# A decoder block's start with x loaded twice: by token for the sums of squares, by feature for the projections

## Chip, cores and metric

The kernel runs on one NeuronCore of one Trainium2 chip. The metric is the device time of one execution in microseconds (us). Before the change the median of three runs is 838.75 us (838.01 to 840.37).

## The reference

One layer of a decoder trunk on 512 tokens of 1024 features, in float32. What matters here is its beginning and one side product:

```python
h = rmsnorm(x, g_pre_mix)                  # x * rsqrt(mean(x*x over features) + 1e-6) * g
ca, cb, q, k, v, pu, gl = split_cols(h @ w_in)
...
bias = rel_bias[rel_bucket(dist)]          # added to the attention logits
...
x = x + sigmoid(x @ w_ple_gate) * (p @ w_ple_proj)
```

The whole of `h @ w_in` waits for the RMS norm, the norm for the sum over all features of each token's squares. `p @ w_ple_proj` needs no norm and only the embedding `p`.

## The kernel before

All activations lie with features on the partitions and the 512 tokens along the free axis: `x` is eight tiles `x_t[kt]` of 128x512, 256 KB each. Weights come as chunks of 128x1024 (512 KB, `raw`), in the order in which they are used. Each chunk is split by ScalarE into a rounded high part `wh` (line 90, a cast) and by VectorE into the low rest `wl` (line 94). Activations are split in the same way by `mul_split` (lines 149 and 150). A product then takes three matmuls, high by high, high by low and low by high (`mm3`, lines 154 to 156).

The part up to `start.close()` stands in an order written by hand; behind it a scheduler with a simulated time line places the instructions, and it may put them anywhere between the hand-ordered ones that it follows. Each engine executes its own list strictly in its order, so an instruction that waits holds everything behind it on its engine. SyncE (SP) issues nearly all loads, GpSimd (POOL) the stores `proj_d` to DRAM and the copies of the attention bias.

The start goes like this. Eight warm-up matmuls (line 192) run while the first data travel. SP issues half of chunk 0, the two tiles of `p`, the other half, four tiles of `x`, half of chunk 1, four tiles of `x`, the other half, then the small parameters `par_sb` (128x493, line 177), `rb_sb` and `oh_sb` (lines 178 and 179, the bias table and its one-hot selector), then chunks 2 and 3. TensorE computes `p @ w_ple_proj` from chunks 0 and 1 (`project_p`, eight output tiles of six matmuls, 48 in all). Meanwhile ScalarE squares each tile of `x` and VectorE adds the squares (`add_square`). The sum over features is a sum over partitions, so TensorE makes it with a column of ones (line 211, in `rstd_steps`), VectorE scales the result, GpSimd raises it to the power -1/2 (line 203), and four transposes by TensorE (line 216) spread it over the partitions. Then, tile by tile, VectorE multiplies `x_t[kt]` by it (line 336), and `mul_split` makes `xnh` and `xnl`, the two parts of the normed input, with the gains from `par_sb`.

The first real use of the normed input is one q tile and one k tile, computed side by side from chunks 2 and 3: 48 matmuls, six for each `kt`, so that each `kt` can start as soon as its `xnh` and `xnl` are there. Ahead of them in TensorE's list stands one small matmul (line 373) that makes the rows of the attention bias from `oh_sb` and `rb_sb`; ScalarE copies them to `rel_r` and GpSimd sends them to DRAM. The scalars of the attention (`lam_s`, `lam_t`, `sub_g`, lines 355 to 368) are computed by VectorE from `par_sb`.

Two limits are written out: `N_RAW` = 3 buffers for raw chunks (a chunk's load waits until the chunk three before it is split; `rel_r` takes a turn in the same three), and at most eight loads of SP in flight, since each waits for the one eight before it.

Of the kernel before, what the change touches and what calls it, by code (L numbers as in the profile page):

```python
# [11 lines left out]
AF = mybir.ActivationFunctionType  # L12
ALU = mybir.AluOpType
# [8 lines left out]

NORM_LAG, WAIT_SUB, WAIT_LN = 10, 4, 8


X_BEFORE_W1, W_EARLY, XN_BEFORE_W3, XN_BEFORE_W4, N_WARM = 3, 2, 2, 7, 8


PACE_OUT, PACE_IN, W_AHEAD = (6, 11), (9, 14), 3
# [5 lines left out]
P = 128  # L35
S = 512
HALF = 256
D = 1024
KT = 8
# [3 lines left out]
EPS = 1e-6  # L43
# [5 lines left out]
DW_W = 32  # L49
# [5 lines left out]
NPAR = CINV + 64  # L55
# [56 lines left out]
def block_kernel(ctx: ExitStack, tc: tile.TileContext, xT, pT, wts, pool_w, par, rel_bias, onehot, out):  # L112
    nc = tc.nc
# [12 lines left out]
    W = Weights(tc, wts, rawp, hlp)  # L126
# [26 lines left out]
    def mm3(o, sh, sl, mh, ml, first, last):  # L153
        nc.tensor.matmul(out=o, lhsT=sh, rhs=mh, start=first, stop=False)  # L154
        nc.tensor.matmul(out=o, lhsT=sh, rhs=ml, start=False, stop=False)  # L155
        nc.tensor.matmul(out=o, lhsT=sl, rhs=mh, start=False, stop=last)  # L156


    start = ExitStack()
    start.enter_context(tc.manual_schedule())  # L160
    p_sb = [act_tile("p") for _ in range(2)]
    x_t = [act_tile("x") for _ in range(KT)]
    par_sb = cp.tile([P, NPAR], F32, name="par_sb")
    rb_sb = cp.tile([32, NH], F32, name="rb_sb")
# [12 lines left out]
    nc.sync.dma_start(out=par_sb, in_=par)
    nc.sync.dma_start(out=rb_sb, in_=rel_bias)
    nc.sync.dma_start(out=oh_sb, in_=onehot)
    W.load(3)  # L180
    mean_mat = cp.tile([P, P], F32, name="mean_mat")
    nc.vector.memset(mean_mat, 1.0 / S)
    ident = cp.tile([P, P], F32, name="ident")
# [3 lines left out]
    neghalf = cp.tile([P, 4], F32, name="neghalf")  # L187
# [18 lines left out]
    def rstd_steps(sq, lo, n, inv_n, got, tag="at"):  # L206


        b = bank(tag)
        for j in range(n):  # L210
            nc.tensor.matmul(out=b[:, j:j + 1], lhsT=sq[:, lo + j * P:lo + (j + 1) * P], rhs=ones_col,  # L211
                             start=True, stop=True)
        r = rstd_from(b[:, 0:n], inv_n, n, "pe")
        yield
        for j in range(n):
            nc.tensor.transpose(out=b[:, j * P:(j + 1) * P], in_=r[:, j:j + 1].to_broadcast([P, P]), identity=ident)  # L216
        got(b[:, 0:n * P])
# [57 lines left out]
    LEFT, RIGHT = slice(0, 512), slice(512, 1024)  # L275
# [4 lines left out]
    p_hl = []  # L280
# [2 lines left out]
        mul_split(h, l, p_sb[kt])  # L283
        p_hl.append((h, l))
    W.split(0, RIGHT)
    ssum = act_tile("ssum")

    def add_square(kt):
        if kt == 0:
            nc.scalar.activation(out=ssum, in_=x_t[0], func=AF.Square)  # L290
        else:
            q = act_tile("sq")
            nc.scalar.activation(out=q, in_=x_t[kt], func=AF.Square)
            nc.vector.tensor_tensor(out=ssum, in0=ssum, in1=q, op=ALU.add)

    proj_d = dr.tile([KT, P, S], F32, name="proj_d")
    banks = {}
# [1 line left out]
    def project_p(m):  # L299
        wh, wl = W.tiles[m // 4]  # L300
        b = banks[m] = bank("mm" if m < 4 or m > 5 else "at")
        for kt in range(2):
            c0 = ((m % 4) * 2 + kt) * P
            mm3(b, wh[:, c0:c0 + P], wl[:, c0:c0 + P], *p_hl[kt], kt == 0, kt == 1)

    stores = []

    def keep_p(m):
        t = act_tile("proj")
        nc.scalar.activation(out=t, in_=banks.pop(m), func=AF.Copy, scale=0.5)  # L310
        stores.append((m, t))

    for m in range(4):
        project_p(m)
        add_square(m)
    for kt in range(4, KT):
        if kt == X_BEFORE_W1 + 1:
            W.split(1, LEFT)
        add_square(kt)
    project_p(4)  # L320
    project_p(5)
    keep_p(0), keep_p(1)
    W.split(1, RIGHT)
    chunk[0] = 2
    x_rB = []
    steps = rstd_steps(ssum, 0, 4, 1.0 / D, x_rB.append)
    next(steps)
    project_p(6)
    W.upto(W_EARLY)
    keep_p(2), keep_p(3)  # L330
    next(steps, None)
    project_p(7)
    xn = []
    for kt in range(KT + 1):
        if kt < KT:
            nc.vector.tensor_tensor(out=x_t[kt], in0=x_t[kt], in1=x_rB[0], op=ALU.mult)  # L336
        if kt > 0:
            h, l = act_tile("xnh", F32R, "xn", xnp), act_tile("xnl", F32R, "xn", xnp)
            mul_split(h, l, x_t[kt - 1], pcol(G_PRE_MIX + kt - 1))
            xn.append((h, l))  # L340
        if kt == XN_BEFORE_W3:
            W.upto(3)
        if kt == XN_BEFORE_W4:
            W.upto(4)
    for m in range(4, KT):
        keep_p(m)
    for m, t in stores:
        nc.gpsimd.dma_start(out=proj_d[m], in_=t)


    lam_t = cp.tile([P, 8], F32, name="lam_t")
# [20 lines left out]
    b = bank("at")  # L372
# [10 lines left out]
                                                      ap=[[0, P], [1, 640]]))  # L383

    repeat_rows(0)

    start.close()


    def project(n, evac, side_by_side=False):  # L390
# [329 lines left out]
    for what in ORDER:  # L720
# [17 lines left out]
        else:  # L738
            m = at_m[what]
# [26 lines left out]
    x_t = []  # L766
# [142 lines left out]
    for quarter in range(4):  # L909
# [58 lines left out]
def _layout(inp):  # L968
    import numpy as np
    g = {k: np.asarray(v) for k, v in inp.items()}  # L970
    f = np.float32

    def feat(a, n):
        return np.ascontiguousarray(a.T.reshape(n, P, S).transpose(1, 0, 2))

    def tiles(w):

        k, m = w.shape
        return w.reshape(k // P, P, m // P, P).transpose(2, 1, 0, 3)

    w_in = g["w_in"][0]
    cols = lambda a, n: w_in[:, a:a + n]
    m_tiles = lambda w: [t.reshape(P, -1) for t in tiles(w)]
    conv_a, conv_b = m_tiles(cols(0, 512)), m_tiles(cols(512, 512))
    q, k = m_tiles(cols(1024, 512)), m_tiles(cols(1536, 512))
    pool = m_tiles(cols(2560, 512))
    gates = m_tiles(cols(3072, 3072))
    v = cols(2048, 512).reshape(KT, P, 512).transpose(1, 0, 2)

    def pairs(w, n):  # L990
        t = tiles(w)
        return [t[i:i + n].transpose(1, 0, 2, 3).reshape(P, -1) for i in range(0, len(t), n)]

    ch = pairs(g["w_ple_proj"][0], 4)
    n_conv = n_qk = 0
    done = [0, 0, 0]
    ys = [pairs(g[n][0], 2) for n in ("w_conv_out", "w_attn_out", "w_pool_out")]
    for what in ORDER:
        if what == "v":
            ch += [v[:, 2 * j:2 * j + 2].reshape(P, -1) for j in range(4)]  # L1000
        elif what == "pool":
            ch += pool
        elif what == "conv":
# [12 lines left out]
    ch += m_tiles(g["w_out"][0])
    w1 = m_tiles(g["w_mlp_in"][0])
    for i in range(4):
        ch += w1[8 * i:8 * i + 8] + m_tiles(g["w_mlp_out"][0][1024 * i:1024 * i + 1024])
    ch += m_tiles(g["w_ple_gate"][0])  # L1020
    wts = np.ascontiguousarray(np.stack(ch))

    par = np.zeros((P, NPAR), f)
    vec = lambda a: a.reshape(-1, P).T
    for c, n in ((G_PRE_MIX, "g_pre_mix"), (G_POST_MIX, "g_post_mix"), (G_PRE_MLP, "g_pre_mlp"),
                 (G_POST_MLP, "g_post_mlp")):
        par[:, c:c + 8] = vec(g[n][0])
    dw = g["conv_dw_w"][0][:, 0, :]
    par[:, DW_W:DW_W + 4 * CW] = dw.reshape(CW, 4, P).transpose(2, 1, 0).reshape(P, -1)
    for c, n in ((DW_B, "conv_dw_b"), (LN_G, "conv_ln_g"), (LN_B, "conv_ln_b"), (POOL_S, "pool_scale")):  # L1030
        par[:, c:c + 4] = vec(g[n][0])
    par[:, SUBLN] = g["subln_g"][0]
    par[:, LAM:LAM + 256] = g["lam_p"][0].reshape(1, 256)
    for i, w in enumerate(WINDOWS):
        par[:, CINV + 16 * i:CINV + 16 * i + 16] = (f(1.0) / np.minimum(np.arange(16) + 1, w).astype(f))[None]

    onehot = np.zeros((32, S), f)
    onehot[_rel_bucket(S - 1 - np.arange(S)), np.arange(S)] = 1.0
    return [feat(g["x"][0], KT), feat(g["p"][0, 0], 2), wts,
            np.ascontiguousarray(g["pool_w"][0].transpose(1, 0, 2).reshape(P, S)), par, np.ascontiguousarray(g["rel_bias"]), onehot]  # L1040


# [25 lines left out]
```

## Time and profile before

| What | us |
|---|---|
| median of 3 runs | 838.75 (838.01 to 840.37) |
| the profiled execution, its own time | 839.83 |
| its span from first to last instruction | 838.1 |
| TensorE busy | 830.9 (99%) |
| VectorE busy | 505.4 (60%) |
| ScalarE busy | 348.6 (42%) |
| GpSimd busy | 30.0 (4%) |

The span is divided among engines that work at the same time, so the shares add up to more than one. TensorE is busy nearly throughout, and the chain that ended last goes through it for 97% of the span. The first 45 us are where the change acts; the rows for them stand further down. Matmul ends are modelled, so neighbouring matmuls overlap in the rows: the distance from start to start tells the pace.

### The profile page before, as it was taken

To read this page: it belongs to the slowest core of one execution; us is meant where nothing else is said; L and a number is where in the kernel's file an instruction comes from. 1 tells how busy PE (TensorE), PEld (TensorE's weight loads), DVE (VectorE), ACT (ScalarE), POOL (GpSimd) and SP (SyncE) were. 2 spreads that over 40 slices of the span, in tenths; PEclk is the share of its full clock that TensorE was granted. 3 is DMA by queue.
4 is the path that set the end of the run, shared out by engine and by line. 5 is a ranking of instruction groups with operands and counts; after the bars stand their busy time and mean duration, and the time that the engine had idled before them with its cause. 6 is when DMAs were issued, how large, how long until landed. Compare 5 with 4: busy or idle time off the path is not lost.

```text
span 838.1 us, 10679 instructions
## 1 busy us (share of the span) xinstructions
PE 830.9 (99%) x4180; PEld 703.6 (84%) x4180; DVE 505.4 (60%) x835; ACT 348.6 (42%) x564; POOL 30.0 (4%) x66
## 2 busy tenths in 40 slices
PE   8999999999999999999999999999999999999998
PEld 7788888888888888888999888888888888889997
DVE  5869669965679985675387631443334434435772
ACT  6734635555452323752446542342233223425341
POOL 2210000010000000000000000000000000000000
PEclk9999999999999999999999999999999999999999
DMA  7463322222222232265203423322223222222311
GB/s 270 152 235 112 113 101 76 79 87 75 76 76 78 99 100 82 95 220 181 76 27 119 158 83 118 101 97 82 98 101 101 100 81 97 100 76 76 127 59 68
DMA packets 27523, 89.11 MB, mean 106 GB/s; under 512 B 3244, under 2 KB 3628, under 8 KB 27472
## 3 DMA queue, kind: packets, MB, share of 16 engines
q1 hardware_dynamic: 26160, 83.95, 29.7%
q0 software_dynamic: 1312, 4.47, 1.6%
q8 instruction: 33, 0.54, 0.3%
q14 instruction: 18, 0.15, 0.1%
HBM read 84.20 MB, written 5.52 MB: 107 GB/s over the span
## 4 chain that ended last, share of the span: by engine, by line
PE 97%; DVE 1%; ACT 0%; DMA 0%; POOL 0%; issue 0%; SPq 0%; ACTq 0%
PE mm L154 21%; PE mm L156 21%; PE mm L155 21%; PE at L154 10%; PE at L155 10%; PE at L156 10%; PE at L211 1%; PE at L457 1%; PE at L455 1%; PE at L488 1%; PE at L216 0%; DMA p<-in_pT_dram 0%; DVE wl L94 0%; POOL per L203 0%; DVE x L336 0%; DVE xnl L150 0%
## 5 line engine op out<-in xcount | busy, mean ns | idle before, releaser
L90 ACT CAST wh<-raw 128x1024 fp32r<-128x1024 f32 (+1 forms) x144 | 148.8, 1038 | 331.2 <-PE mm L155 151.7
L94 DVE TENSOR_TENSOR wl<-raw,wh 128x1024 fp32r<-128x1024 f32 (+1 forms) x144 | 173.3, 1208 | 100.7 <-ACT wh L90 100.3
L156 PE MATMUL mm<-xnh,wl 128*128 128x512 f32 x352 | 137.9, 392 | 0.5 <-DVE wl L94 0.4
L155 PE MATMUL mm<-xnl,wh 128*128 128x512 f32 x352 | 137.6, 391 | 0.0
L154 PE MATMUL mm<-xnh,wh 128*128 128x512 f32 x352 | 137.2, 393 | 0.0
L577 DVE SCALAR_TENSOR_TENSOR acc<-u,par_sb,acc 128x512 f32<-128x512 f32 x116 | 81.3, 742 | 1.2 <-ACT acc L571 1.1
L156 PEld LDWEIGHTS mm<-xnh,wl 128*128 128x128 f32 x352 | 66.1, 188 | 14.6 <-DVE wl L94 1.4
L154 PEld LDWEIGHTS mm<-xnh,wh 128*128 128x128 f32 x352 | 66.1, 188 | 14.2 <-ACT xnh L149 0.9
L155 PEld LDWEIGHTS mm<-xnl,wh 128*128 128x128 f32 x352 | 66.1, 188 | 14.1 <-DVE xnl L150 0.4
L154 PE MATMUL mm<-sh,wh 128*128 128x512 f32 (+1 forms) x152 | 54.4, 358 | 0.0
L155 PE MATMUL mm<-sl,wh 128*128 128x512 f32 (+1 forms) x152 | 54.4, 358 | 0.0
L156 PE MATMUL mm<-sh,wl 128*128 128x512 f32 (+1 forms) x152 | 54.3, 357 | 0.0
L154 PE MATMUL at<-sh,wh 128*128 128x512 f32 (+1 forms) x144 | 53.1, 369 | 0.0
L155 PE MATMUL at<-sl,wh 128*128 128x512 f32 (+1 forms) x144 | 53.0, 368 | 0.0
L156 PE MATMUL at<-sh,wl 128*128 128x512 f32 (+1 forms) x144 | 52.9, 368 | 0.0
L154 PE MATMUL at<-xgh,wh 128*128 128x512 f32 (+1 forms) x144 | 52.8, 367 | 0.0
L155 PE MATMUL at<-xgl,wh 128*128 128x512 f32 (+1 forms) x144 | 52.7, 366 | 0.0
L154 PE MATMUL mm<-xgh,wh 128*128 128x512 f32 (+1 forms) x144 | 52.7, 366 | 0.0
L156 PE MATMUL mm<-xgh,wl 128*128 128x512 f32 (+1 forms) x144 | 52.7, 366 | 0.0
L156 PE MATMUL at<-xgh,wl 128*128 128x512 f32 (+1 forms) x144 | 52.7, 366 | 0.0
L155 PE MATMUL mm<-xgl,wh 128*128 128x512 f32 (+1 forms) x144 | 52.6, 366 | 0.0
L203 POOL TENSOR_TENSOR per<-pec,neghalf 128x4 f32<-128x4 f32 (+1 forms) x11 | 12.3, 1120 | 581.1 <-DVE pec L201 581.1
(251 smaller groups left out, 1537.9 us busy)
## 6 DMA issues: line engine op xcount, KB each, us to landing
raw<-in_wts_dram SPq DMA_DIRECT2D x140, 512.0 KB, 3.2
x<-in_xT_dram SPq DMA_DIRECT2D x16, 256.0 KB, 5.7
proj_d<-proj POOLq DMA_DIRECT2D x8, 256.0 KB, 4.0
proj<-proj_d SPq DMA_DIRECT2D x8, 256.0 KB, 3.9
out_dram<-pg SPq DMA_DIRECT2D x7, 256.0 KB, 2.0
rep_d<-rel_d POOLq DMA_DIRECT2D x4, 320.0 KB, 8.2
raw<-in_wts_dram SPq DMA_DIRECT2D x4, 256.0 KB, 5.2
bias<-rep_d POOLq DMA_DIRECT2D x4, 256.0 KB, 4.1
```

The source lines that it names most:

```text
L90: i = self.nc.scalar.copy(out=wh[:, sl], in_=src)
L94: i = self.nc.vector.tensor_tensor(out=wl[:, sl], in0=src, in1=wh[:, sl].bitcast(F32), op=ALU.subtract)
L154: nc.tensor.matmul(out=o, lhsT=sh, rhs=mh, start=first, stop=False)
L155: nc.tensor.matmul(out=o, lhsT=sh, rhs=ml, start=False, stop=False)
L156: nc.tensor.matmul(out=o, lhsT=sl, rhs=mh, start=False, stop=last)
L203: nc.gpsimd.tensor_tensor(out=r, in0=c, in1=neghalf[:, 0:n], op=ALU.pow)
L211: nc.tensor.matmul(out=b[:, j:j + 1], lhsT=sq[:, lo + j * P:lo + (j + 1) * P], rhs=ones_col, start=True, stop=True)
L455: nc.tensor.matmul(out=lg[m][:, 0:nn], lhsT=q[m][:, cols], rhs=k[m][:, 0:nn], start=True, stop=False)
L457: nc.tensor.matmul(out=lg[m][:, 0:nn], lhsT=ql[m][:, cols], rhs=k[m][:, 0:nn], start=False, stop=True)
L488: nc.tensor.transpose(out=tp[:, j * P:(j + 1) * P], in_=e[:, j * P:(j + 1) * P], identity=ident)
L577: nc.vector.scalar_tensor_tensor(out=t, in0=u[:, k:k + S], scalar=pcol(w0 + k), in1=t, op0=ALU.mult, op1=ALU.add)
```

## The change

`x` becomes a DRAM tensor of sixteen tiles: the eight by feature as before, and behind them the same numbers with tokens on the partitions. The second eight (`x_k`, 2 MB) are loaded first. For each group of 128 tokens ScalarE squares one half of the features with an accumulated sum, VectorE the other half in one instruction, and the mean of squares is there without TensorE's column of ones. The load of `par_sb` is cut in two: its first 32 columns (the gains) stay early, the other 461 come last, behind all of `x`, `rb_sb` and `oh_sb`. Chunk 2 is loaded ahead of the tiles by feature, chunk 3 in their middle. There is one more warm-up matmul, the three matmuls of `project_p` change places among themselves, six of its eight tiles now precede the transposes, and `start.close()` moves up, so that the attention's scalars and the bias matmul are placed by the scheduler.

```diff
-X_BEFORE_W1, W_EARLY, XN_BEFORE_W3, XN_BEFORE_W4, N_WARM = 3, 2, 2, 7, 8
+K_BEFORE_W1, XN_BEFORE_W3, XN_BEFORE_W4, N_WARM = 1, 3, 7, 9
...
+    x_k = [act_tile("xk") for _ in range(2 * 4)]
...
-    for kt in range(KT):
-        nc.sync.dma_start(out=x_t[kt], in_=xT[:, kt, :])
-        if kt == X_BEFORE_W1:
-            W.load(1, halves=True)
+    W.load(1, halves=True)
+    for j in range(2 * 4):
+        nc.sync.dma_start(out=x_k[j], in_=xT[:, KT + j, :])
+        if j == K_BEFORE_W1:
             W.load_half(1, 0)
     W.load_half(1, 1)
-    nc.sync.dma_start(out=par_sb, in_=par)
-    nc.sync.dma_start(out=rb_sb, in_=rel_bias)
-    nc.sync.dma_start(out=oh_sb, in_=onehot)
-    W.load(3)
+    def load_x(kt):
+        nc.sync.dma_start(out=x_t[kt], in_=xT[:, kt, :])
+    nc.sync.dma_start(out=par_sb[:, 0:DW_W], in_=par[:, 0:DW_W])
+    W.load(2)
+    for kt in range(4):
+        load_x(kt)
...
+    for kt in range(4, KT):
+        load_x(kt)
+        if kt == 4:
+            W.load(3)
+    nc.sync.dma_start(out=rb_sb, in_=rel_bias)
+    nc.sync.dma_start(out=oh_sb, in_=onehot)
+    nc.sync.dma_start(out=par_sb[:, DW_W:NPAR], in_=par[:, DW_W:NPAR])
+    half_ms = small(8, "halfms")
+    for j in range(4):
+        if j == 3:
+            W.split(1, LEFT)
+        xa, xb = x_k[2 * j], x_k[2 * j + 1]
+        nc.scalar.activation(out=xa, in_=xa, func=AF.Square, scale=1.0 / math.sqrt(D), accum_out=half_ms[:, j:j + 1])
+        nc.vector.tensor_tensor_reduce(out=xb, in0=xb, in1=xb, op0=ALU.mult, op1=ALU.add, scale=1.0 / D, scalar=0.0,
+                                       accum_out=half_ms[:, 4 + j:5 + j])
+    x_c, x_r = small(4, "xc"), small(4, "xr")
+    nc.vector.scalar_tensor_tensor(out=x_c, in0=half_ms[:, 0:4], scalar=EPS, in1=half_ms[:, 4:8],
+                                   op0=ALU.add, op1=ALU.add)
+    nc.gpsimd.tensor_tensor(out=x_r, in0=x_c, in1=neghalf, op=ALU.pow)
...
-    steps = rstd_steps(ssum, 0, 4, 1.0 / D, x_rB.append)
+    x_rB = bank("at")
+    for j in range(4):
+        nc.tensor.transpose(out=x_rB[:, j * P:(j + 1) * P], in_=x_r[:, j:j + 1].to_broadcast([P, P]), identity=ident)
...
     for m, t in stores:
         nc.gpsimd.dma_start(out=proj_d[m], in_=t)
+    start.close()
...
     repeat_rows(0)
-
-    start.close()
```

Three places show how the lists of the engines change. The first is SP's, the loads behind the second half of chunk 1 (`raw_108` before, `raw_112` now). Before (`raw_118` and `raw_120` are chunks 2 and 3):

```order
L177 DMA par_sb<-in_par_dram 128x493
L178 DMA rb_sb<-in_rel_bias_dram 32x4
L179 DMA oh_sb_98<-in_onehot_dram 32x512
L76 DMA raw_118<-in_wts_dram 128x1024
L76 DMA raw_120<-in_wts_dram 128x1024
```

And now, further down, where the last of the tiles of `x` are (`raw_168` is chunk 3; ahead of these rows stand the first cut of `par_sb`, chunk 2 and four more tiles of `x`):

```order
L179 DMA x_92<-in_xT_dram 128x512
L75 DMA raw_168<-in_wts_dram 128x1024
L179 DMA x_93<-in_xT_dram 128x512
L179 DMA x_94<-in_xT_dram 128x512
L179 DMA x_95<-in_xT_dram 128x512
L295 DMA rb_sb<-in_rel_bias_dram 32x4
L296 DMA oh_sb_98<-in_onehot_dram 32x512
L297 DMA par_sb<-in_par_dram 128x461
```

`rb_sb`, `oh_sb` and most of `par_sb` moved behind two chunks and the eight tiles of `x`.

The second is VectorE's list around the first two tiles of the normed input. Before:

```order
L336 TENSOR_TENSOR x_88<-x_88,at_232 128x512
L336 TENSOR_TENSOR x_89<-x_89,at_232 128x512
L150 SCALAR_TENSOR_TENSOR xnl_270<-x_88,par_sb,xnh_269 128x512
L336 TENSOR_TENSOR x_90<-x_90,at_232 128x512
L150 SCALAR_TENSOR_TENSOR xnl_275<-x_89,par_sb,xnh_274 128x512
```

And now:

```order
L346 TENSOR_TENSOR x_89<-x_89,at_240 128x512
L370 TENSOR_TENSOR lam_s<-par_sb 128x64 x2
L377 TENSOR_SCALAR sub_g<-par_sb 128x1
L381 TENSOR_SCALAR par_sb<-par_sb 128x124
L383 TENSOR_SCALAR ln_half<-par_sb 128x8
L149 SCALAR_TENSOR_TENSOR xnl_266<-x_88,par_sb,xnh_265 128x512
L346 TENSOR_TENSOR x_90<-x_90,at_240 128x512
L386 MEMSET rel_r 4x640
L371 TENSOR_REDUCE lam_t<-lam_s 128x1 x2
L149 SCALAR_TENSOR_TENSOR xnl_275<-x_89,par_sb,xnh_274 128x512
```

The attention's scalars, which read the late part of `par_sb`, moved from behind the last `xnl` to ahead of the first, and the clearing of `rel_r` with two reductions ahead of the second.

The third is TensorE's list between the last matmuls of `project_p` and the first with the normed input. Before:

```order
L155 MATMUL mm_260<-pl_153,wh_144 128x512
L156 MATMUL mm_260<-ph_152,wl_145 128x512
L373 MATMUL at_349<-oh_sb_98,rb_sb 4x512
L154 MATMUL mm_363<-xnh_269,wh_248 128x512
L155 MATMUL mm_363<-xnl_270,wh_248 128x512
```

And now:

```order
L323 MATMUL mm_252<-ph_161,wl_154 128x512
L323 MATMUL mm_252<-pl_162,wh_153 128x512
L388 MATMUL at_350<-oh_sb_98,rb_sb 4x512
L153 MATMUL mm_363<-xnh_265,wh_260 128x512
L154 MATMUL mm_363<-xnl_266,wh_260 128x512
```

The bias matmul kept its place, ahead of all matmuls with the normed input.

## Rows read from the trace of the kernel before

**Rows 1.** The page's part on busy time, by engine.

```profile
PE 830.9 (99%) x4180; PEld 703.6 (84%) x4180; DVE 505.4 (60%) x835; ACT 348.6 (42%) x564; POOL 30.0 (4%) x66
```

**Rows 2.** Stretches: start:end, length; busy us (instructions) by engine; clock, DMA share, GB/s.

```profile
5.53:10.37 4.84, 4.84 (x11) 3.52 (x12) 2.93 (x5) 3.47 (x6) 0.00 (x0) 1.00 0.95 338
...
22.43:34.01 11.58, 11.46 (x49) 8.88 (x49) 11.21 (x20) 8.06 (x13) 1.70 (x4) 1.00 0.31 96
```

**Rows 3.** Time line of TensorE: start, us, instruction, [idle before <-releaser].

```profile
16.28 0.95 PE L211 MATMUL at<-ones_col,ssum 128*128 128x1 f32 x8
...
19.52 0.65 PE L216 MATMUL at<-ident,per 128*128 128x128 f32 x4 [0.80 <-POOL per L203]
...
21.48 1.02 PE L373 MATMUL at<-oh_sb,rb_sb 32*4 32x512 f32 x2
22.43 0.50 PE L154 MATMUL mm<-xnh,wh 128*128 128x512 f32 x1
...
40.49 0.50 PE L156 MATMUL mm<-xnh,wl 128*128 128x512 f32 x1 [0.42 <-DVE wl L94]
```

**Rows 4.** Time line of SP: when each load is issued, and how many.

```profile
8.66 0.33 SPq L81 DMA_DIRECT2D raw<-in_wts_dram  x1
9.29 0.33 SPq L177 DMA_DIRECT2D par_sb<-in_par_dram  x1
...
10.60 0.32 SPq L179 DMA_DIRECT2D oh_sb<-in_onehot_dram  x1
11.23 1.08 SPq L76 DMA_DIRECT2D raw<-in_wts_dram  x2
```

**Rows 5.** Loads issued in short windows, in their order: KB each, us from issue to landing.

```profile
raw<-in_wts_dram SPq DMA_DIRECT2D x1, 256.0 KB, 5.1
...
par_sb<-in_par_dram SPq DMA_DIRECT2D x1, 246.5 KB, 5.5
...
oh_sb<-in_onehot_dram SPq DMA_DIRECT2D x1, 64.0 KB, 4.5
...
raw<-in_wts_dram SPq DMA_DIRECT2D x1, 512.0 KB, 5.0
```

**Rows 6.** A stretch with loads alone, columns as in rows 2.

```profile
7.40:13.80 6.40, 6.40 (x24) 5.08 (x23) 4.74 (x8) 6.25 (x11) 0.00 (x0) 1.00 1.05 398
```

**Rows 7.** Time line of GpSimd: the power and the first four stores.

```profile
17.52 1.95 POOL L203 TENSOR_TENSOR per<-pec,neghalf 128x4 f32<-128x4 f32 x1 [14.50 <-DVE pec L201]
19.41 2.34 POOL L348 DMA_DIRECT2D proj_d<-proj  x4
```

**Rows 8.** DMA queues from 42 to 52 us (q0 GpSimd's, q1 SP's): MB, share of 16 engines.

```profile
DMA packets 922, 3.51 MB, mean 351 GB/s; under 512 B 128, under 2 KB 128, under 8 KB 922
...
q0 software_dynamic: 400, 1.61, 50.2%
q1 hardware_dynamic: 522, 1.90, 48.9%
```

**Rows 9.** Time line of VectorE, from 10 to 60 us.

```profile
21.69 0.75 DVE L150 SCALAR_TENSOR_TENSOR xnl<-x,par_sb,xnh 128x512 fp32r<-128x512 f32 x1 [0.20 <-ACT xnh L149]
...
32.86 0.21 DVE L355 TENSOR_TENSOR lam_s<-par_sb 128x64 f32<-128x64 f32 x1
33.10 0.22 DVE L356 TENSOR_REDUCE lam_t<-lam_s 128x1 f32<-128x64 f32 x1
...
36.96 0.59 DVE L371 MEMSET rel_r<- 4x640 f32 x1
```

**Rows 10.** Time line of ScalarE: four squares; the copy of the bias rows.

```profile
11.23 2.60 ACT L293 ACTIVATE sq<-x 128x512 f32<-128x512 f32 x4
...
37.64 0.58 ACT L374 COPY rel_r<-at 4x512 f32<-4x512 f32 x1
```

**Rows 11.** End of the span: the last matmul; TensorE's stretch after it, columns as in rows 2.

```profile
833.70 0.28 PE L156 MATMUL at<-x2h,wl 128*128 128x256 f32 x1
...
836.50:838.00 1.50, 0.00 (x0) 0.00 (x0) 0.00 (x0) 0.00 (x0) 0.00 (x0) 0.50 0.05 15
```

More of the change, by code (lines that the diff above doesn't have):

```diff
@@ L285, in block_kernel @@
     W.split(0, RIGHT)
[L286 to L294, printed above, removed]
+    for kt in range(4, KT):
[17 more added lines that the diff above has]
+    nc.gpsimd.tensor_tensor(out=x_r, in0=x_c, in1=neghalf, op=ALU.pow)
     proj_d = dr.tile([KT, P, S], F32, name="proj_d")
@@ L303, in project_p @@
             c0 = ((m % 4) * 2 + kt) * P
-            mm3(b, wh[:, c0:c0 + P], wl[:, c0:c0 + P], *p_hl[kt], kt == 0, kt == 1)
+            for z, (w, src) in enumerate(((wh, 0), (wl, 0), (wh, 1))):
+                nc.tensor.matmul(out=b, lhsT=w[:, c0:c0 + P], rhs=p_hl[kt][src], start=kt + z == 0, stop=kt + z == 3)
     stores = []
@@ L311, in keep_p @@
         stores.append((m, t))
-    for m in range(4):
+    for m in range(6):
         project_p(m)
[L315 to L322, printed above, removed]
-    W.split(1, RIGHT)
-    chunk[0] = 2
-    x_rB = []
-    steps = rstd_steps(ssum, 0, 4, 1.0 / D, x_rB.append)
[L327 to L332, printed above, removed]
+    W.split(1, RIGHT)
+    for m in range(2):
+        keep_p(m)
+    x_rB = bank("at")
+    for j in range(4):
+        nc.tensor.transpose(out=x_rB[:, j * P:(j + 1) * P], in_=x_r[:, j:j + 1].to_broadcast([P, P]), identity=ident)
+    chunk[0] = 2
+    for m in range(6, KT):
+        project_p(m)
     xn = []
@@ L335, in block_kernel @@
         if kt < KT:
-            nc.vector.tensor_tensor(out=x_t[kt], in0=x_t[kt], in1=x_rB[0], op=ALU.mult)
+            nc.vector.tensor_tensor(out=x_t[kt], in0=x_t[kt], in1=x_rB, op=ALU.mult)
+        if kt == 0:
+            W.upto(2)
         if kt > 0:
@@ L340, in block_kernel @@
             xn.append((h, l))
+        if kt == 1:
+            keep_p(2), keep_p(3)
         if kt == XN_BEFORE_W3:
@@ L1038, in _layout @@
     onehot[_rel_bucket(S - 1 - np.arange(S)), np.arange(S)] = 1.0
-    return [feat(g["x"][0], KT), feat(g["p"][0, 0], 2), wts,
+    x_rows = g["x"][0].reshape(4, P, D).transpose(1, 0, 2).reshape(P, 8, S)
+    x_both = np.ascontiguousarray(np.concatenate([feat(g["x"][0], KT), x_rows], axis=1))
+    return [x_both, feat(g["p"][0, 0], 2), wts,
             np.ascontiguousarray(g["pool_w"][0].transpose(1, 0, 2).reshape(P, S)), par, np.ascontiguousarray(g["rel_bias"]), onehot]
```

## The prediction, written before the changed kernel was run

> **What bounds the kernel now.** I read the busy times first: TensorE works 830.9 of 838.1 us [rows 1], so all that can be won or lost lies in its few gaps and slow stretches. The stretches of the start come next [rows 2]: between 5.53 and 10.37 us eleven matmuls take 4.84 us, 0.44 each, and from 22.43 to 34.01 us 49 take 11.46, 0.234 each. The first is the pace at 1.2 GHz, the second at 2.4. Then TensorE's time line [rows 3]: the column of ones at 16.28, an idle 0.80 us until GpSimd's power is done, the transposes at 19.52, the bias matmul at 21.48, and at 22.43 the first matmul with the normed input. Behind that it runs nearly without a gap until 40.49, where it had waited 0.42 us for a split of VectorE.
>
> So before the change the start can give back little: the ones (0.95 at most), the idle 0.80 and that 0.42. What can be lost has no such bound: the bias matmul and VectorE's list now stand behind late loads. When the loads land decides the case, and the rows on loads [rows 4 to 8] are the ones to read.
>
> **The squares and the power** leave the path, but buy nothing by themselves. A square by ScalarE took 0.65 [rows 10], and there are four on each engine in place of eight on ScalarE and seven sums on VectorE. I take each at 0.65 to 0.85 for the accumulated sum, an estimate from that row. They follow the loads: the last tile by token stands just ahead of chunk 1's second half, which landed at 8.66 + 5.1 = 13.8 [rows 4, 5]. So it lands near 13.2, its square is done near 14.1, the power, at 1.95 [rows 7], near 16.2. TensorE needs it after 36 matmuls of the embedding, which ended at 16.28 before [rows 3] and end there again: the same loads in the same order feed them. Four transposes (0.65 at most [rows 3]) and twelve matmuls at 0.234 [rows 2] follow without a wait: done near 19.6. Were everything else in place, the bias matmul (0.95, from 21.48 to 22.43 [rows 3]) would let the first normed matmul start at 20.6, 1.9 earlier than before. The ninth warm-up matmul and the other order of the three matmuls lie ahead of this and move nothing.
>
> **The loads.** Up to chunk 1's second half the list carries the same bytes as before: 13.8. Behind it now come 3.2 MB up to `oh_sb`, where there were 0.3 MB. In a stretch with loads alone the chip moved 398 GB/s [rows 6], 0.66 us for a tile of 256 KB. Chunk 2 landed at 11.23 + 5.0 = 16.2, `oh_sb` just before it at 10.60 + 4.5 = 15.1 [rows 4, 5], so a chunk takes 1.13; `par_sb` landed at 9.29 + 5.5 = 14.8, 1.0 after what precedes it, and `rb_sb` and `oh_sb` took 0.3 together. The new sum: 13.8 + 0.15 for the first cut of `par_sb` (0.04 by its 16 KB, 0.3 by the row of `oh_sb`) + two chunks at 1.13 + eight tiles at 0.66 + 0.3 = 21.8 for `oh_sb`, and 22.8 for the late `par_sb`.
>
> That is without the stores. The first four of `proj_d` (256 KB each) were issued from 19.41 on, when no load was in flight [rows 7]; now the first two follow the power at 16.2, the next two near 19, in the midst of the loads. From 42 to 52 us both queues were at work: they divided the engines 50.2 to 48.9, at 351 GB/s together [rows 8]. So the price lies between nothing (all loads first) and 3.4 us (all four stores pass ahead: 2.1 MB at 351 instead of 1.05 MB at 398). I take 2.0, nearer to the upper end, since rows 8 show even sharing but the last two stores start late: **`oh_sb` at 23.8, `par_sb` at 24.8.** The Trainium skill says the same in "DMA: Bandwidth & Descriptors", "Issuing engines are not separate DMA queues": DMAs of all engines run on the same 16 DMA engines and interleave. By that rule the stores cost their full bytes, so 2.6 rather than 2.0, and rows 8 agree with it.
>
> **What waits for them.** TensorE executes its list in order, so the bias matmul waits for `oh_sb` from 19.6 to 23.8, 4.2 us, and all normed matmuls behind it. VectorE waits at `lam_s` for the late `par_sb`; behind it stand the first low part `xnl` and all the rest. Four small instructions (0.21 for a `lam_s` [rows 9], overlapping, 0.6 together) put the first `xnl` at 25.4, against 21.69 [rows 9]: **3.7 late**. The clearing of `rel_r` (0.59) and two reductions (0.22, 0.3 for both [rows 9]) now precede the second `xnl`: **0.9 more**. Then VectorE goes on as before, a product and an `xnl` for each of eight tiles and the split of chunk 3; it was busy 11.21 of those 11.58 us [rows 2], so it cannot catch up, and TensorE ends the first q and k pair 4.6 late. It does not get this back: later it is busy throughout. One stall goes: the wait at 40.49, since the copy of the bias rows (37.64 [rows 10]), which held ScalarE's next cast, and the small work of VectorE are over by then: **minus 0.4**. That makes 4.2. Ends: 1.6 + 0.9 - 0.4, about 2.2, without any store ahead, 5.6 with all four at 351 GB/s.
>
> **The clock.** The last matmul of the span ended at 833.98, and in the stretch from 836.5 on the clock is 0.50, 1.2 GHz [rows 11]: it fell within 2.5 us of the last matmul. TensorE will stand still for 4.2 us from 19.6 and then get a few matmuls at a time until about 28. I take it that it falls to 1.2 GHz there and comes back after a steady stretch like that of the start, eleven matmuls at 0.44 instead of 0.234 [rows 2]: 2.3 us, of which 0.5 pass while VectorE is waited for anyway: **plus 1.8**. Ends: 0 if it stays up, 4 if half pace lasts twice as long. The Trainium skill's "TensorE: Matmul & The Clock Gate" ("HAM oscillation") tells of kernels in which each wait for a DMA between bursts of matmuls brings half rate back; the row at the end of this span agrees.
>
> **Sum.** 3.7 + 0.9 - 0.4 + 1.8 = 6.0. The profiled execution took 839.83, 1.7 around its span, and would take 845.8; it lies 1.1 above the median of the runs. Against that median: 838.75 + 6.0, so **844.7**.
>
> **Rivals.**
> - The waits come, but the clock stays at 2.4 GHz, because the bias matmul and the small bursts are enough. For it: the idle 0.80 at 18.7 changed nothing in the pace [rows 2, 3]. 4.2 us, 843.0.
> - The stores wait behind the loads and the clock stays: `par_sb` at 22.8, 2.2 us, 841.0. Against it: rows 8.
> - Not slower: the loads land before they are missed. It is decided at the bias matmul: `oh_sb` has to be there by 19.6 and the late `par_sb` by 21.1, 0.6 ahead of the first `xnl` of before. Then the normed matmuls start 1.9 earlier and the stall of 0.4 is gone; with a little of the moved 0.9 left over, some 2 us are won: 836.8. Against it: 3.2 MB in the 5.8 us from 13.8 would be 550 GB/s, and rows 6 show 398.
> - The part that the words of the change promise does not happen: the token sums come no sooner, for the squares wait for the same 2 MB as before. That is worth nothing either way, since TensorE waits for `oh_sb` until long after the power.
>
> **How the numbers follow.** The forecast, waits and a fallen clock, gets 0.55, the waits alone 0.27, the light case at 841.0 0.12, the faster case 0.06. A measurement of this kernel tells about 0.3% from no change, 2.5 us: slower begins at 841.3, faster at 836.2. So the first two are slower (0.82, less a little for sizes that come out small), the light case and most of the faster one are within it. The range of 8 in 10 reaches from just under the light case, 840.8, to 847.0, where all four stores pass ahead or the clock comes back late.
>
> **What would show it.** In the changed profile: the bias matmul at about 24 instead of 21.48, after an idle stretch of some 4 us that ends with a DMA; VectorE idle until `lam_s` at about 25, also for a DMA; GpSimd's power before 16.5; the wait of 0.42 near 40 gone or smaller; matmuls at 0.44 apart again somewhere between 23 and 33; the first matmul of the tile after the q and k pair at about 40, against 34.01; and every stretch after 50 us as before, only later. I am wrong if `oh_sb` lands before 20, if VectorE doesn't wait at `lam_s`, or if the late start is won back further on.

## The result and the profile after

The changed kernel takes **844.68 us** (median of 6 runs, 843.77 to 846.38) against 839.12 (838.01 to 840.37, 6 runs) for the kernel before: ratio 1.0069, 95% interval 1.0056 to 1.0081. It is slower by 5.6 us. The profiled execution took 844.38, with a span of 842.6. Over a whole span the mean granted clock is 0.996 in two of the six executions (844.38, the profiled one, and 843.77) and 0.993 in the other four (843.92 to 846.38).

The page's line of busy times, which answers to [rows 1], shows TensorE with as much work as before and 4.5 us more span around it:

```profile
PE 830.0 (99%) x4174; PEld 703.2 (83%) x4174; DVE 503.1 (60%) x836; ACT 346.4 (41%) x564; POOL 29.1 (3%) x66
```

The stretches, with the columns of [rows 2], say where that is:

```profile
22.43:34.01 11.58, 8.13 (x23) 4.85 (x24) 7.80 (x20) 3.69 (x7) 1.96 (x4) 0.71 0.42 155
24.05:30.87 6.82, 4.99 (x9) 2.36 (x10) 4.66 (x14) 2.82 (x5) 0.40 (x1) 0.50 0.28 115
34.01:45.43 11.42, 11.42 (x52) 9.46 (x51) 8.96 (x12) 10.04 (x16) 5.00 (x11) 1.00 0.90 284
```

From 22.43 to 34.01, where 49 matmuls ran before, there are 23, at a mean clock of 0.71; the clock is 0.50, 1.2 GHz, from 24.05 to 30.87. From 34.01 on TensorE is full again. Its time line, for [rows 3]:

```profile
16.46 0.60 PE L339 MATMUL at<-ident,xr 128*128 128x128 f32 x4
...
19.45 0.40 PE L323 MATMUL mm<-pl,wh 128*128 128x512 f32 x1
25.88 1.86 PE L388 MATMUL at<-oh_sb,rb_sb 32*4 32x512 f32 x2 [6.04 <-DMA oh_sb<-in_onehot_dram]
27.67 0.79 PE L153 MATMUL mm<-xnh,wh 128*128 128x512 f32 x1
...
31.89 0.40 PE L153 MATMUL mm<-xnh,wh 128*128 128x512 f32 x1
32.13 0.39 PE L155 MATMUL mm<-xnh,wl 128*128 128x512 f32 x1
...
40.34 0.39 PE L153 MATMUL mm<-xnh,wh 128*128 128x512 f32 x1
...
51.22 0.39 PE L153 MATMUL mm<-wh,xnh 128*128 128x512 f32 x1
```

The transposes no longer wait for the power, and the last matmul of the embedding starts at 19.45. Then TensorE stands for 6.04 us until `oh_sb` is there. 32.13 is the first matmul with the low part of chunk 3, and 40.34 the first one behind the q and k pair, which stood at 34.01 before: 6.33 later. No wait of 0.42 follows. 51.22 is the first matmul of the work behind the next q and k pair. Before, it stood here:

```profile
45.65 0.39 PE L154 MATMUL mm<-wh,xnh 128*128 128x512 f32 x1
```

So the next pair took 10.88 (40.34 to 51.22) instead of 11.64 (34.01 to 45.65): the stall, 0.42 by its row, is worth 0.76 from start to start, and 5.57 of the 6.33 are left. The last matmul starts only 4.62 later (838.32 against 833.70 [rows 11]). The way there from 51.22 took 787.10 us, from 45.65 it took 788.05, and in the traces of the runs below 787.1 to 787.9 with the close in either place; so this looks like spread between executions, and the medians keep 5.6.

VectorE, for [rows 9]:

```profile
26.13 0.36 DVE L370 TENSOR_TENSOR lam_s<-par_sb 128x64 f32<-128x64 f32 x2 [6.61 <-DMA par_sb<-in_par_dram]
...
26.68 0.74 DVE L149 SCALAR_TENSOR_TENSOR xnl<-x,par_sb,xnh 128x512 fp32r<-128x512 f32 x1
...
28.09 0.59 DVE L386 MEMSET rel_r<- 4x640 f32 x1
28.61 0.27 DVE L371 TENSOR_REDUCE lam_t<-lam_s 128x1 f32<-128x64 f32 x2
28.81 0.73 DVE L149 SCALAR_TENSOR_TENSOR xnl<-x,par_sb,xnh 128x512 fp32r<-128x512 f32 x1
...
30.73 1.21 DVE L93 TENSOR_TENSOR wl<-raw,wh 128x1024 fp32r<-128x1024 f32 x1
```

It waits 6.61 us at `lam_s` for the late cut of `par_sb`; the first `xnl` comes at 26.68 instead of 21.69 [rows 9]. The last row is the split of chunk 3. Two rows of VectorE in the kernel before belong beside these, the second `xnl` and its split of chunk 3:

```profile
22.95 0.75 DVE L150 SCALAR_TENSOR_TENSOR xnl<-x,par_sb,xnh 128x512 fp32r<-128x512 f32 x1
23.62 1.22 DVE L94 TENSOR_TENSOR wl<-raw,wh 128x1024 fp32r<-128x1024 f32 x1
```

GpSimd, for [rows 7], and SP's last small loads, for [rows 4]:

```profile
14.79 1.03 POOL L311 TENSOR_TENSOR xr<-xc,neghalf 128x4 f32<-128x4 f32 x1 [11.77 <-DVE xc L309]
15.80 1.29 POOL L362 DMA_DIRECT2D proj_d<-proj  x2
19.32 1.07 POOL L362 DMA_DIRECT2D proj_d<-proj  x2 [2.23 <-ACT proj L329]
```

```profile
17.67 0.34 SPq L296 DMA_DIRECT2D oh_sb<-in_onehot_dram  x1
18.32 0.35 SPq L297 DMA_DIRECT2D par_sb<-in_par_dram  x1
```

`oh_sb` is issued at 17.67 and used at 25.88; four stores and the last tiles of `x` share the DMA engines with it.

### The profile page after: what moved, and what is told of

The parts are those of the page before. It is cut to its first block, busy times and chain, and to the rows that moved or that the text cites. A ratio compares the mean times of both kernels' runs of the same rounds, so it can differ in the third digit from the quotient of the medians.

```text
span 842.6 us, 10669 instructions
## 1 busy us (share of the span) xinstructions
PE 830.0 (99%) x4174; PEld 703.2 (83%) x4174; DVE 503.1 (60%) x836; ACT 346.4 (41%) x564; POOL 29.1 (3%) x66
## 4 chain that ended last, share of the span: by engine, by line
PE 96%; DMA 3%; DVE 0%; SPq 0%; issue 0%; ACT 0%
PE mm L153 21%; PE mm L154 21%; PE mm L155 21%; PE at L153 10%; PE at L154 10%; PE at L155 10%; DMA oh_sb<-in_onehot_dram 1%; DMA xk<-in_xT_dram 1%; PE at L216 1%; DMA x<-in_xT_dram 1%; PE at L470 1%; PE at L468 1%; PE at L501 1%; DMA p<-in_pT_dram 1%; PE at L221 0%; PE at L388 0%
## 5 line engine op out<-in xcount | busy, mean ns | idle before, releaser
L153 PEld LDWEIGHTS mm<-sh,wh 128*128 128x128 f32 x152 | 28.5, 188 | 4.5
```

## The experiments

The theory was that of the prediction: TensorE waits for `oh_sb` and VectorE, at the moved `lam_s`, for the late `par_sb`; the stores make both loads later, and the clock adds to it. The rivals: the double load of `x` itself costs, or one of the waits is harmless. Each kernel was run in five rounds beside the kernel before, whose medians then were 838.5 to 838.9. The edits are against the changed kernel, if nothing else is said; a mark for all of them is the start of the first matmul behind the pair (34.01 before, 40.34 in the change). The table's numbers are those of the paragraphs below; runs 3, 4 and 9 to 11 have other edits and stand only there.

| Kernel | small loads | close of the first pool | median us | ratio to before (95%) |
|---|---|---|---|---|
| the change | `oh_sb`, `par_sb` last | moved up | 844.68 | 1.0056 to 1.0081 |
| 2 | `oh_sb`, `par_sb` last | old place | 843.25 | 1.0040 to 1.0064 |
| 5 | `oh_sb` early, `par_sb` last | moved up | 846.28 | 1.0078 to 1.0109 |
| 6 | `oh_sb` early, `par_sb` last | old place | 837.93 | 0.9984 to 1.0001 |
| 1 | all early | moved up | 844.90 | 1.0058 to 1.0082 |
| 7 | all early | old place | 839.06 | 0.9993 to 1.0010 |
| 8 | those of before, `x` once | moved up | 843.72 | 1.0053 to 1.0085 |

**1. All small parameters early.**

```diff
     nc.sync.dma_start(out=par_sb[:, 0:DW_W], in_=par[:, 0:DW_W])
+    nc.sync.dma_start(out=rb_sb, in_=rel_bias)
+    nc.sync.dma_start(out=oh_sb, in_=onehot)
+    nc.sync.dma_start(out=par_sb[:, DW_W:NPAR], in_=par[:, DW_W:NPAR])
     W.load(2)
```

> The changed kernel with rb_sb, oh_sb and the late cut of par_sb loaded right behind the first cut, ahead of chunk 2 and of x by feature; x is still loaded twice. If the wait for these small loads is the cause, the bias matmul starts near 19.7 us instead of 25.9, VectorE does not stop for lam_s, and the time falls from 844.7 to between 838 and 840.5. If the second load of x itself is the cause (x by feature lands too late), the normed matmuls only wait elsewhere and the time stays at 842.5 or more.

Measured 844.90: a miss. The scheduler, which now saw `par_sb` early, put `lam_s` still further ahead, in front of chunk 0's second split. VectorE waits there, and TensorE for the split, first VectorE's row and then TensorE's:

```profile
14.83 0.36 DVE L370 TENSOR_TENSOR lam_s<-par_sb 128x64 f32<-128x64 f32 x2 [7.46 <-DMA par_sb<-in_par_dram]
```

```profile
15.85 0.80 PE L323 MATMUL mm<-ph,wl 128*128 128x512 f32 x1 [6.32 <-DVE wl L93]
```

So a wait had only changed its place, and this run can't tell what the loads cost.

**2. The old close.**

```diff
-    start.close()
...
     repeat_rows(0)
+
+    start.close()
```

> The changed kernel with start.close() back at its old place: the attention's scalars and the clearing of rel_r stand behind the last xnl on VectorE, the loads are as in the change. If VectorE's wait at lam_s is the bound, the normed matmuls come early and the time falls to 840 or less. If TensorE's wait for oh_sb is enough by itself, the bias matmul still starts near 25.9, the first normed matmul near 27.7, the q and k pair ends near 40, and the time is 844 to 845.5.

Measured 843.25, between the two forecasts. `lam_s` stands behind the last `xnl` again and waits for nothing, but TensorE still stands before the bias matmul:

```profile
23.88 1.86 PE L387 MATMUL at<-oh_sb,rb_sb 32*4 32x512 f32 x2 [4.43 <-DMA oh_sb<-in_onehot_dram]
25.67 0.79 PE L153 MATMUL mm<-xnh,wh 128*128 128x512 f32 x1
...
38.58 0.39 PE L153 MATMUL mm<-xnh,wh 128*128 128x512 f32 x1
...
45.06 0.50 PE L155 MATMUL mm<-xnh,wl 128*128 128x512 f32 x1 [0.42 <-DVE wl L93]
```

So most of the loss is there without any wait at `lam_s`: the wait for `oh_sb` makes it, together with the clock that falls in it. The clock's part: the bias matmul takes 1.79 us to the next start, 0.95 before [rows 3], and the 48 matmuls of the pair 12.91 (25.67 to 38.58) instead of 10.95 at 0.228 (the pace of the change from 32.13 to the mark), together 2.8. The wait itself ends only 2.40 later than the bias matmul of before. And the stall of 0.42 is back, as it should be if the moved work of VectorE and ScalarE had removed it.

**3. The stores last.**

```diff
-    for m, t in stores:
+    for m, t in reversed(stores):
```

> The changed kernel with the eight stores of proj_d issued in reverse, so that GpSimd sends none before the bias rows: no store shares the DMA engines with the loads. If the stores delay the loads, oh_sb lands near 22 instead of 25.7 and par_sb near 23, and the time falls by some 3 us, to 841 to 842.5. If they wait their turn behind the loads, nothing moves: 844 to 845.

The tile that is ready last now heads the stores, and the others stand behind it in GpSimd's list, so all of them follow the loads. Measured 843.14 (ratio 1.0037 to 1.0061): below the change, but short of the 841 to 842.5 expected. TensorE and VectorE:

```profile
22.86 1.01 PE L388 MATMUL at<-oh_sb,rb_sb 32*4 32x512 f32 x2 [3.51 <-DMA oh_sb<-in_onehot_dram]
...
38.97 0.39 PE L153 MATMUL mm<-xnh,wh 128*128 128x512 f32 x1
```

```profile
23.15 0.36 DVE L370 TENSOR_TENSOR lam_s<-par_sb 128x64 f32<-128x64 f32 x2 [4.09 <-DMA par_sb<-in_par_dram]
...
27.75 1.21 DVE L93 TENSOR_TENSOR wl<-raw,wh 128x1024 fp32r<-128x1024 f32 x1
```

Both waits end 3.0 us earlier (25.88 to 22.86, 26.13 to 23.15), but the pair only 1.37. The stretches up to the bias matmul, of the change and of this kernel, and then the slow one of this kernel:

```profile
14.35:25.74 11.39, 5.49 (x26) 4.15 (x25) 3.36 (x7) 4.96 (x8) 3.37 (x5) 0.93 1.03 390
```

```profile
14.35:22.73 8.38, 5.01 (x24) 3.77 (x22) 3.11 (x4) 4.59 (x8) 0.97 (x1) 1.00 1.03 390
24.63:31.46 6.83, 6.27 (x14) 4.41 (x15) 6.76 (x14) 4.11 (x7) 2.37 (x5) 0.50 0.22 76
```

The DMA engines move 390 GB/s with and without the stores. The loads ran 0.5 us ahead here by themselves (chunk 1's second half was issued at 8.71, and at 9.20 in the change), so some 2.5 of the 3.0 us are the stores'. At that rate this is 0.98 MB, and GpSimd's queue moved 1.05 MB, all four stores, in the stretch of the change. So stores that pass ahead cost about their bytes, but how many pass differs between executions: with them `oh_sb` took 8.1 us from issue to landing in the change, 7.8 in run 11, 6.5 in run 2 and 6.4 in run 4, and without them 5.2 here. The rest of what this won is lost in the slow stretch: from the end of chunk 3's split to the mark it takes 10.01 us here (28.96 to 38.97), 8.40 in the change (31.94 to 40.34).

**4. Matmuls that fill the wait.** 26 more matmuls stand before the bias matmul, into its bank, which it then overwrites.

```diff
+    rel_b = bank("at")
+    for _ in range(N_FILL):
+        nc.tensor.matmul(out=rel_b, lhsT=W.tiles[1][0][:, 0:P], rhs=p_hl[0][0], start=True, stop=True)
...
-    b = bank("at")
+    b = rel_b
```

> The changed kernel with 26 matmuls of 128x512 on operands that are there already, between the last one of the embedding and the bias matmul; their result is overwritten. They fill the wait for oh_sb, so the clock should stay at 2.4 GHz. By the prediction's term of 1.8 us for the clock the time falls to about 842.9; by the changed kernel's own rows, where VectorE's pace hides most of the slow stretch, by 0.5 only, to about 844.2. The landing of oh_sb stays near 25.7.

Measured 843.90, ratio 1.0070 (1.0053 to 1.0086). The profiled execution (843.75) has a clock of 1.00 throughout the start. TensorE, and VectorE's split of chunk 3:

```profile
25.07 1.02 PE L393 MATMUL at<-oh_sb,rb_sb 32*4 32x512 f32 x2
...
30.98 0.50 PE L157 MATMUL mm<-xnh,wl 128*128 128x512 f32 x1 [0.17 <-DVE wl L95]
...
39.28 0.39 PE L155 MATMUL mm<-xnh,wh 128*128 128x512 f32 x1
```

```profile
29.72 1.21 DVE L95 TENSOR_TENSOR wl<-raw,wh 128x1024 fp32r<-128x1024 f32 x1
```

From the end of the split (30.93) to the mark it is 8.35 us, against 8.40 in the change with its slow stretch: in the profiled execution of the change the fallen clock costs 0.05 us. (`oh_sb` was there at 23.5 here, so the 26 matmuls themselves held the bias matmul; the mark doesn't suffer, since TensorE still waits for the split.)

The 0.05 is not the price of every execution. In the change the last of the twelve matmuls that don't need the split starts at 31.89, and the split ends at 31.94; so the slow stretch was only just short enough, and four of the six executions have a lower mean clock. With the filler the four executions at 0.999 or 1.00 took 843.31 to 844.04; the two in which the clock fell, 0.997 and 0.996, took 844.90 and 847.69 and raise the ratio. The medians lie 5.0 us above the kernel before here, and 5.6 in the change.

**5. `oh_sb` early, the close as in the change.** `rb_sb` and `oh_sb` are loaded behind the first cut of `par_sb`.

```diff
     nc.sync.dma_start(out=par_sb[:, 0:DW_W], in_=par[:, 0:DW_W])
+    nc.sync.dma_start(out=rb_sb, in_=rel_bias)
+    nc.sync.dma_start(out=oh_sb, in_=onehot)
     W.load(2)
```

> The change with rb_sb and oh_sb loaded right behind the first cut of par_sb and nothing else moved: the late cut of par_sb stays last, and the close of the first pool stays where the change put it, so that the bias matmul has nothing to wait for and lam_s stands in front of the first xnl. My theory (two waits lie side by side, and each alone is enough): lam_s waits for the late cut until 25 to 26.8 us, TensorE's first normed matmul on an xnl comes at 26 to 27.5, its first matmul after the pair at 39 to 41.5, and the time is 843 to 845.5. Rival (the loss is the wait for oh_sb, and lam_s adds only its 0.9 us on VectorE): the time is 838 to 839.5.

Measured 846.28: the theory's side, and beyond its range. TensorE, VectorE from `lam_s` on, and the slow stretch:

```profile
19.32 1.02 PE L388 MATMUL at<-oh_sb,rb_sb 32*4 32x512 f32 x2
20.27 0.51 PE L153 MATMUL mm<-xnh,wh 128*128 128x512 f32 x1
28.30 0.80 PE L154 MATMUL mm<-xnl,wh 128*128 128x512 f32 x1 [7.53 <-DVE xnl L149]
...
42.09 0.39 PE L153 MATMUL mm<-xnh,wh 128*128 128x512 f32 x1
```

```profile
26.96 0.36 DVE L370 TENSOR_TENSOR lam_s<-par_sb 128x64 f32<-128x64 f32 x2 [7.30 <-DMA par_sb<-in_par_dram]
...
31.56 1.21 DVE L93 TENSOR_TENSOR wl<-raw,wh 128x1024 fp32r<-128x1024 f32 x1
```

```profile
23.51:33.75 10.24, 4.97 (x11) 3.48 (x12) 6.71 (x17) 3.20 (x6) 0.86 (x2) 0.50 0.32 127
```

With the wait for `oh_sb` gone, TensorE stands for 7.53 us one matmul later, for the first `xnl`. `lam_s` came 0.83 later than in the change, and from the end of the split (32.77) to the mark it took 9.32 instead of 8.40: the clock stayed at half for 10.24 us here, beyond the split, and for 6.82 in the change. 0.83 and 0.92 are the 1.75 by which the mark is later. The mean clock of this execution is 0.993, that of four executions of the change; so in those the fallen clock costs some 0.9, an estimate from this run.

**6. `oh_sb` early and the old close.** The edits of 5 and 2 together; the late cut of `par_sb` is still last, and `x` is still loaded twice.

> The double load of x stays; rb_sb and oh_sb are loaded right behind the first cut of par_sb, the late cut of par_sb stays last, and the close of the first pool stands at its old place, so that lam_s and its followers stay behind the normed tiles. My theory (the loss is the wait for oh_sb, and what the scheduler moved in front of the normed tiles): the bias matmul no longer waits, the first normed matmul starts at 20.2 to 21.5 us, TensorE's first matmul after the normed pair at 32 to 33.5, and the time is 837 to 839, 1 to 2 under the kernel before. Rival (loading x twice costs by itself, since the feature tiles x5 to x7 then land near 23 to 25 us and hold up the normed pair): the first normed matmul is early, but TensorE waits over 1.5 us in all on the later xnl between 21 and 35 us, and the time is 840 or more.

Measured 837.93: as expected, and no different from the kernel before within the measurement. TensorE, and VectorE's split of chunk 3:

```profile
19.13 1.02 PE L387 MATMUL at<-oh_sb,rb_sb 32*4 32x512 f32 x2
20.07 0.51 PE L153 MATMUL mm<-xnh,wh 128*128 128x512 f32 x1
...
23.72 0.50 PE L153 MATMUL mm<-xnh,wh 128*128 128x512 f32 x1 [0.92 <-ACT wh L89]
...
33.27 0.39 PE L153 MATMUL mm<-xnh,wh 128*128 128x512 f32 x1
```

```profile
23.70 1.23 DVE L93 TENSOR_TENSOR wl<-raw,wh 128x1024 fp32r<-128x1024 f32 x1 [0.66 <-ACT wh L89]
```

The whole loss is gone without a change to the double load, so that rival falls; what is left of it is TensorE's wait of 0.92 for chunk 3. The first normed matmul starts 2.36 us earlier than before, the mark only 0.74: chunk 3 is split at 23.70, as before at 23.62, behind one more tile and a load that comes later.

**7. All early and the old close.** The edits of 1 and 2 together.

> As the run with all small parameters loaded right behind the first cut, but with the close of the first pool at its old place, so that lam_s no longer stands ahead of chunk 0's split. My theory: TensorE's stop for that split at 15 us is gone, no small load is waited for, and the time is 837 to 839.5, some 5 to 7 under the run with the same loads and the moved close. Rival (the 250 KB of late parameters ahead of chunk 2 and x delay the normed pair themselves): 841 or more, with TensorE waiting for x tiles or for chunk 2 between 20 and 26 us.

Measured 839.06, as expected. Run 1, with the same loads and the close moved up, took 5.8 us more; its wait of 7.46 at `lam_s` is absent here.

**8. The kernel before with the close moved up, and nothing else.**

```diff
         nc.gpsimd.dma_start(out=proj_d[m], in_=t)
+    start.close()
...
     repeat_rows(0)
-
-    start.close()
```

> The kernel before with one line moved: the close of the first pool stands ahead of the lambda work, as in the change; the loads are those of before. It tells what the moved close costs by itself. My theory (moving lam_s and its followers ahead costs their own 0.9 us of VectorE where VectorE sets the pace, and nothing waits for a load, since par_sb has landed by then): 838.5 to 840, within 0.3% of the kernel before. Rival (the moved order alone holds TensorE up, whatever the loads): 840.5 or more.

Measured 843.72: a miss, on the rival's side. I had taken it that `par_sb` is there when `lam_s` comes. But the scheduler put `lam_s` between the sums of the squares, and VectorE came to it before the load had landed. VectorE's row, and TensorE's:

```profile
15.56 0.22 DVE L356 TENSOR_TENSOR lam_s<-par_sb 128x64 f32<-128x64 f32 x1 [3.75 <-DMA par_sb<-in_par_dram]
```

```profile
17.05 0.50 PE L156 MATMUL at<-ph,wl 128*128 128x512 f32 x1 [4.04 <-DVE wl L94]
```

So with three orders of loads in which nothing waits for `oh_sb` the moved close costs 5.0 us (here), 5.8 (run 1 against 7) and 8.4 (run 5 against 6), each time with a wait of VectorE at `lam_s` for `par_sb`. In the change, where TensorE waits for `oh_sb` at the same time, it adds 1.4 (against run 2).

**9. Run 6 with the stores last** (the edit of 3 added).

> As the run with rb_sb and oh_sb early and the old close, and the eight stores of the projected embedding are issued in reverse order on POOL, so that none shares the DMA engines with the loads of x and of chunk 3. My theory (the loads of the last x tiles are slowed by the stores by about 1 us, and the last of them are near the path): x7 lands 1 to 1.5 us earlier, and the time is 0 to 1 under that run: 836.5 to 838.5. Rival (the normed pair is paced by VectorE, not by loads): the same time as that run within 0.3 us, and x7 earlier all the same; or slower by up to 1, if the late stores hold up the load of a bias on the same queue.

Measured 838.07 (0.9985 to 1.0003), the same as run 6: the rival's time.

**10. Run 9 with the tiles 0 and 1 of `x` loaded ahead of chunk 2.**

> The run with rb_sb and oh_sb early, the old close and the stores in reverse order, with one more edit: feature tiles 0 and 1 of x are loaded ahead of chunk 2, since VectorE stood 2.2 us for the first of them there and then works through to the last xnl. My theory (from there VectorE's 18 operations set the end of the normed pair): the first x times rstd starts at 16.5 to 17.3 us instead of 18.0, the first matmul after the pair comes at 32 to 33, and the time is 836.5 to 838, 0 to 1 under the run without the edit. Rival (chunk 2 now lands 0.7 to 1.4 later and its split holds VectorE up by as much): the same time as that run within 0.4 us, with a wait for chunk 2's wh in VectorE's row behind the first x times rstd.

Measured 840.04 (1.0006 to 1.0024): slower than run 9, beyond both forecasts. The rival's mechanism is there; VectorE starts on `x` earlier and then stands for chunk 2:

```profile
16.48 0.69 DVE L348 TENSOR_TENSOR x<-x,at 128x512 f32<-128x512 f32 x1 [1.00 <-PE at L341]
19.43 1.22 DVE L93 TENSOR_TENSOR wl<-raw,wh 128x1024 fp32r<-128x1024 f32 x1 [2.26 <-ACT wh L89]
```

Part of the loss is the clock: seven of the eleven executions have a mean of 0.998 and took 839.74 to 841.08, the four at 1.00 took 838.12 to 839.81.

**11. Run 2 with 18 matmuls that fill the wait** (the edits of 2 and 4).

> The run with the old close (oh_sb late, lam_s back behind the last xnl), with 18 more matmuls in front of the bias matmul that fill most of the wait for oh_sb and are overwritten. My theory (a fallen clock costs nothing while VectorE sets the pace, as in the change, but much where TensorE itself has all its operands waiting, as in the run with the old close: 2.8 us there): the bias matmul starts at 23.5 to 25.5 us, the clock stays at 1.00 from there, the first matmul after the normed pair comes 11.9 to 12.3 us behind the start of the bias matmul (14.7 in the run without the filler), and the time is 840 to 841.5. Rival (the clock's price is small here too, and what is lost is the wait alone): 842.5 to 843.5, with the first matmul after the pair over 13.5 us behind the bias matmul.

Measured 840.13 (1.0011 to 1.0034), as the theory expected: 3.1 us under run 2, which differs by the filler alone. The profiled execution was one of the longer ones (843.2): there `oh_sb` came 1.68 us behind the last filler, the clock fell after all, and 13.6 us passed from the bias matmul to the mark. So the profile doesn't show the shorter time to the mark that the theory names. But the mean granted clock of each execution tells it: 0.999 or 1.00 in ten of the twelve, which took 839.77 to 841.35, and 0.998 and 0.995 in the two long ones, 843.2 and 845.2. All five of run 2 have 0.996 and took 842.9 to 843.68. So of the 4.4 us that run 2 loses the fallen clock makes about 3, and the wait for `oh_sb` with the clock up 1.5.

## Why the prediction was right

The time was right, 844.7 said and 844.68 measured. That it agrees so closely is luck: 6.0 us were added to a median of 838.75 from three runs, and the shift measured is 5.6, against 839.12 from six. By its steps, against the trace of the profiled execution (positive is later):

| Step of the prediction | said | measured |
|---|---|---|
| the wait for `oh_sb` ends | 23.8 | 25.88 |
| the wait for the late `par_sb` ends | 24.8 | 26.13 |
| first `xnl` | +3.7 | +4.99 |
| work moved ahead of the second `xnl` | +0.9 | +0.87 |
| split of chunk 3 one tile later | not priced | +0.34 |
| the clock | +1.8 | +0.05 |
| the stall at 40.49 | -0.4 | -0.76 |
| sum | +6.0 | +5.49 |

The mark in the two traces gives 6.33 less the stall's 0.76, so 5.57, and the medians of the runs 5.6. The stall's size recurs: the next pair takes 10.88 or 10.89 where the close is moved up (runs 3, 4 and 5) and 11.60 where it isn't (runs 2, 6 and 7).

- **The waits** came where they were said, TensorE's before the bias matmul and VectorE's at `lam_s`, and both ended 1.3 to 2.1 us later than said. 0.5 to 1.0 of it was the term for the stores: 2.0 taken, 2.5 to 3.0 by run 3. The Trainium skill says in "DMA: Bandwidth & Descriptors", "Issuing engines are not separate DMA queues", that the DMAs of all engines run on the same 16 DMA engines and interleave. The rows of run 3 agree: 390 GB/s with and without the stores. The prediction's 2.6 for the full bytes came nearer than its 2.0 in this execution, in which all four stores passed; over the traces the delay of `oh_sb` is 1.2 to 2.9, and both lie in it.
- **The moved work** was as said: the second `xnl` is 5.86 later, the first 4.99.
- **What I overlooked** is that chunk 3 is now split behind the third `xnl`, not the second: 1.25 later against the second `xnl` (30.73 less 28.81, against 23.62 less 22.95). Of that, 0.91 is given back: 39 matmuls of the pair were left from the first use of that split before (9.12 us), and 36 are now (8.21).
- **The clock** is the term that was mis-sized. It fell to 1.2 GHz, as the prediction has it, but "plus 1.8" added its loss to VectorE's delay, and the two lie side by side: at half pace TensorE still got through what VectorE gave it, and it was back at 2.4 GHz before the split of chunk 3 ended, behind which it runs without a wait. By run 4 the price is 0.05 in the profiled execution. In the four executions with the lower mean clock it is some 0.9, by the estimate from run 5; that is not measured in the change itself. Where TensorE is itself the bound, as in run 2, it is large: 2.8 by its trace, and run 11 won 3.1 there. The prediction took the pace at half clock, 0.44, from the stretch of 5.53 to 10.37, whose row gives a clock of 1.00 [rows 2]; the slow stretch of run 3, 14 matmuls in 6.27 us at 0.50, is 0.45 each and bears its pace out.
- So the right total has two errors in it that nearly cancel in this execution: waits too short by 1.3, a clock too dear by 1.75. The split not seen (0.34) and the stall (0.36 more won than said) cancel as well. To that extent the total was luck; the path, two waits side by side and the later one deciding, was right.
- **The squares and the power** buy nothing, as said, while the loads are late. Run 6, where neither small load is waited for, gains 0.74 us at the mark.
- **The rivals.** "The waits come, but the clock stays" came near the price of the clock in the profiled execution, though the clock did fall, and had its waits too short: 843.0. The faster case asked for the small loads to be in time. Run 6 makes that so, and gives 837.93 where 836.8 was said, because the split of chunk 3 then sets the pace.
- The prediction let the later of the two waits decide. The table of runs bears that out: with `oh_sb` early alone (run 5) the loss stays, `lam_s` moved back alone (run 2) takes 1.4 off it, and both together (run 6) take all.

## What to carry to other kernels

When a change hands instructions to a scheduler, read on each engine what they now stand in front of and which load they wait for: small work whose operands land late can cost more than the transfer that was the point of the change. When two engines wait side by side, mending one wait shows little (runs 2 and 5), so mend both before judging the loads. Price a fallen clock only on the stretch in which TensorE has its operands and sets the pace: about 3 us in run 2, 0.05 in the profiled change. And look at the mean clock of every execution, not of the profiled one alone.

## What the runs showed that was not expected

- The fall of the clock cost 0.05 us in the profiled change, 0.9 in run 5, 1.6 in run 3 and about 3 in run 2. Half pace lasted 6.8 us in the change, in run 3 and in run 2, and 10.24 in run 5. What differs between the first three is how much work with all its operands there lay before TensorE while the clock was low.
- The power by GpSimd on a tile of 128x4 took 1.03 us in the change and 1.95 before [rows 7]. No run settles why.
- Loads in the same order end at different times in different executions: the wait for `oh_sb` ended at 23.88 in the profiled execution of run 2 and at 25.26 in that of run 11, whose loads and stores are the same. Up to then the stores had moved 0.68 of their 1.05 MB in run 2 and all of it in run 11. A landing that sets the time should be read with a margin of a microsecond or more.
